# FFN of a two-layer decoder trunk: more places for the first weight parts, later first down products, later splits of kept halves, and a last tile run once

## Chip, cores and metric

The kernel runs on one core of a Trainium2 chip. The metric is the device time of one execution in microseconds (us). Five engines run their own instruction streams: TensorE (PE, with its weight loads shown as PEld), VectorE (DVE), ScalarE (ACT), GpSimd (POOL) and SyncE (SP, which here only issues DMAs). Each executes its stream in order and waits on semaphores of the others. An L with a number is a line of the kernel before, and in rows of the changed kernel a line of that.

## What is computed

One inference step of two layers, each a token mixer (an mLSTM in layer 0, latent attention over a paged cache in layer 1) followed by a SwiGLU FFN, for 1024 prompt tokens and 8 single new tokens with the same weights. All is float32. The change touches the FFN alone:

```python
def swiglu(x, w_gate_up, w_down):          # x (.., 1024), w_gate_up (1024, 5632), w_down (2816, 1024)
    g, u = jnp.split(x @ w_gate_up, 2, axis=-1)
    return (jax.nn.silu(g) * u) @ w_down
...
        hp = hp + swiglu(rmsnorm(hp, norm_ffn[layer]), ffn_w_gate_up[layer], ffn_w_down[layer])
        hs = hs + swiglu(rmsnorm(hs, norm_ffn[layer]), ffn_w_gate_up[layer], ffn_w_down[layer])
...
    y_prompt = rmsnorm(hp, norm_final)
    y_sample = rmsnorm(hs, norm_final)
```

## The kernel before

**Numbers in two halves.** Each operand of a matmul is split into a high and a low half: ACT copies it to the matmul type (L117, the hi), DVE subtracts that from the source (L118, the lo). A product is three matmuls, hi by hi (L134), hi by lo (L135) and lo by hi (L136).

**Tiles.** The 2816 hidden columns are 22 tiles f of 128, the tokens two halves i, in the matmuls 256 and 260 columns wide. The normalised input stands in SBUF as seven forms per half (sums and differences of its quarters), split too: names f0 to f7 for half 0, c0 to c5 and again f7 for half 1. `forms` makes them.

**Gate and up.** For one tile the gate and up columns together are four blocks a11, a12, a21, a22, and seven products of sums of blocks with the forms do the work of eight (`PRODUCTS`, in the order a11, a12, S2, s1, s3, a22, S4, with s1 = a21 + a22, S2 = s1 − a11, S4 = a12 − S2, s3 = a11 − a21). `operands` loads the blocks as two raw tiles of 512 KB, tag `wr`, which has two buffers. SP issues these loads at L994. POOL makes s1 (L1007), s3 (L1008), S2 in place of s1 (L1012) once s1 is split, and S4 in place of S2 (L1015) once S2 is split. Each of the seven *parts* is split into a weight tile of its own. Three places take turns: two buffers of tag `wh` and one of tag `w3`. `gate_up` runs the seven products for each token half given in `parts`, and asks `operands` for one part ahead of the one in use. A third pair, tag `wl`, stands beside `wh` in the same pool; the mixers use it, the gate and up products here do not.

**Order of the tiles.** While `forms` still makes half 1, `gate_up_half` runs tiles 0 and 1 for half 0 alone. Then `ffn` runs tile 2 for both halves, tiles 0 and 1 for half 1, and tiles 3 to 17 for both. In between it hands out the *down products* of the first 18 tiles: `down` is a generator of 504 steps, each three matmuls into banks mm and ss, with a piece of DVE or ACT work that empties a bank or prepares a next operand (b from the hidden values u; dA to dD from w_down, raw tile dr). `gate_up` has a *checkpoint* after every second group of three matmuls, 28 in a tile for both halves, and takes steps there: 2 each in tile 3 from the second checkpoint on, 1 each in the tiles behind. The two buffers `st0` of `down` have tag `wl`.

**The last four tiles** (18 to 21) are not fed to `down`: `keep` splits their hidden values (L117, out a) for `last_products`, which the end of the layer runs (`to_mla` after layer 0, `finish` after layer 1, with weight tiles wh and fw from w_down). In layer 1 tile 21 is run as two calls, one per token half, each with loads, sums and splits of its own.

A list scheduler orders the instructions of each engine when the kernel is built; on the chip that order is fixed.

Of the kernel before, what the change touches and what calls it, by code (L numbers as in the profile page):

```python
# [28 lines left out]
NF = DFF // P  # L29
# [62 lines left out]
class Kern:  # L92
# [896 lines left out]
    def operands(self, wg, f):  # L989
        nc = self.nc  # L990
        A = []
        for c0 in (f * P, DFF + f * P):
            raw = self.t(self.wp, [P, KT * P], "wr")
            nc.sync.dma_start(raw.rearrange("p (k m) -> p k m", m=P), self.wsrc(wg, 0, KT, c0, P))  # L994
            A.append(raw.rearrange("p (k r m) -> p r k m", r=2, m=P))
        (a11, a12), (a21, a22) = ((x[:, 0], x[:, 1]) for x in A)

        def put(x):
            self.no += 1
            pool, tag = (self.wp, "wh") if self.no % 3 else (self.gu, "w3")  # L1000
            w = self.t(pool, [P, KT * P], tag, F32R).rearrange("p (i k m) -> p i k m", i=2, m=P)
            self.split(w[:, 0], w[:, 1], x)
            return w

        G = nc.gpsimd.tensor_tensor
        s, s3 = (self.t(self.gu, [P, 4, P], "S", bufs=2) for i in range(2))
        G(s, a21, a22, op=ALU.add)  # L1007
        G(s3, a11, a21, op=ALU.subtract)  # L1008
        yield put(a11)
        yield put(a12)  # L1010
        s1 = put(s)
        G(s, s, a11, op=ALU.subtract)  # L1012
        yield put(s)
        yield s1
        G(s, a12, s, op=ALU.subtract)  # L1015
        yield put(s3)
        yield put(a22)
        yield put(s)


    def gate_up(self, wg, f, parts, down=iter(()), skip=0, steps=1):
        nc = self.nc
        V = nc.vector
        gu = self.gu
        banks = {}
        U, X = {}, {}
        ops = self.operands(wg, f)
        ahead = next(ops)
        for s, bank, first in PRODUCTS:
            w, ahead = ahead, next(ops, None)  # L1030
            for i in parts:
                pw = PW[i]
                if (i, bank) not in banks:
                    banks[i, bank] = self.mmt("sc")[:, :pw]
                ps = banks[i, bank]
                xh, xl = self.F[i][s]
                for k in range(4):
                    self.mm3(ps, w[:, 0, k], w[:, 1, k], xh[:, k], xl[:, k], bool(first) and k == 0, k == 3, skip_group_check=True)
                    if k % 2:
                        if skip:  # L1040
                            skip -= 1
                        else:
                            for _ in range(steps):
                                next(down, None)
                if s == 0:
                    U[i] = self.rows(f, i)
                    X[i] = self.t(gu, [P, PW[1]], "gt", bufs=2)[:, :pw]
                u, x = U[i], X[i]
                if s == 0:
                    nc.scalar.copy(u[:, 0], ps)  # L1050
                elif s == 4:
                    V.tensor_tensor(u[:, 0], u[:, 0], ps, op=ALU.add)
                    nc.scalar.activation(u[:, 0], u[:, 0], AF.Silu)
                elif s == 3:
                    nc.scalar.copy(x, ps)
                elif s == 2:
                    nc.scalar.copy(u[:, 1], ps)
                    V.tensor_tensor(u[:, 1], u[:, 1], banks[i, 1], op=ALU.add)
                elif s == 5:
                    V.tensor_tensor(u[:, 0], u[:, 0], ps, op=ALU.mult)  # L1060
                elif s == 6:
                    V.tensor_tensor(x, x, ps, op=ALU.add)
                    nc.scalar.activation(x, x, AF.Silu)
                    V.tensor_tensor(u[:, 1], u[:, 1], x, op=ALU.mult)  # L1064
# [92 lines left out]
    def ffn(self, layer):  # L1157
        wg, wd = self.ffn_w_gate_up[layer], self.ffn_w_down[layer]
        self.fp = self.pool("ffn")
        self.B = {}  # L1160
        for _, x, i in SPREAD:
            if i == 0:
                self.spread(0, x, i)
        self.gate_up(wg, 2, (0, 1))
        self.gate_up(wg, 0, (1,))
        self.gate_up(wg, 1, (1,))
        for _, x, i in SPREAD:
            if i == 1:
                self.spread(0, x, i)
        g = self.down(wd)  # L1170
        next(g)
        self.gate_up(wg, 3, (0, 1), g, 1, 2)
        for f in range(4, NF - 2):
            self.gate_up(wg, f, (0, 1), g)
        for _ in g:
            pass
        self.fp.release()
        self.fp = self.pool("ffn2")
        fs = range(NF - 4, NF)
        self.act = {f: [self.t(self.fp, [P, T], "a%d%d" % (f % 4, x), F32R) for x in range(2)] for f in fs}  # L1180

        def keep(f, i):
            o = lambda x: x[:, 512 * i:512 * i + 2 * PW[i]].rearrange("p (c t) -> p c t", c=2)
            self.split(o(self.act[f][0]), o(self.act[f][1]), self.u[f, i])

        for f in fs[:2]:
            for i in range(2):
                keep(f, i)
        for f in fs[2:]:
            for parts in ((0,), (1,)) if layer and f == NF - 1 else ((0, 1),):  # L1190
                self.gate_up(wg, f, parts)
                for i in parts:
                    keep(f, i)
        self.fc.release()
        return wd, fs

# [820 lines left out]
```

## Time and profile before

| | us |
|---|---|
| median of 3 timed runs | 2763.43 (2760.77 to 2763.75) |
| the profiled execution | 2736.87, its span 2735.1 |
| mean granted PE clock in it | 0.972 |
| tiles 2, 0, 1 of layer 0's FFN, up to the first steps of `down` | 557.1 to 617.1 |
| tile 3 of layer 0 | 617.1 to 655 |
| last tile of layer 0 (both halves at once) | 1174.0 to 1194.1 |
| tiles 2, 0, 1 of layer 1's FFN | 2023.7 to 2082.5 |
| last tile of layer 1 (half by half) | 2639.2 to 2669.8 |

A row of the profile reads: start, duration, engine, line, operation, output<-inputs by the program's names, and in brackets how long the engine stood idle before it and what ended the wait. Names stand without their numbers: `sc` is a PSUM bank of the gate and up products, `mm` and `ss` are banks of the down products, `S` is a sum that POOL makes, `wh`, `wl`, `w` (for w3) are split weight parts.

### The profile page before, as it was taken

The numbers are of one execution on the slowest core, as the hardware profiler recorded it, in microseconds if no ns is written. First come the engines' busy times: TensorE is split into PE (matmuls) and PEld (weight loads), VectorE is DVE, ScalarE is ACT, GpSimd is POOL, SyncE is SP. The second block draws the span as 40 slices with busy tenths as digits, with TensorE's granted clock in tenths as the row PEclk, the third lists the DMA queues.
The fourth block names the chain that finished last, engine by engine and source line by source line (L and its number), as shares of the span: only waits on it lengthen the run. The fifth ranks groups of instructions, "written<-read, shape, count | busy, mean of one in ns | idle before, by whom it ended". The sixth has DMA issues, their size and how long they took to land. (4 is left out here: it accounts for less than half of the span.)

```text
span 2735.1 us, 54524 instructions
## 1 busy us (share of the span) xinstructions
PE 2553.6 (93%) x21151; PEld 2398.4 (88%) x21151; DVE 1884.8 (69%) x4321; ACT 1320.8 (48%) x3287; POOL 824.9 (30%) x762
## 2 busy tenths in 40 slices
PE   8999998979999999999889889888989999999988
PEld 8998976979999999999877677677988999999988
DVE  4345668868777778666558777685676877777755
ACT  4212334446555555454345464555345555555542
POOL 1000102223333333322336454442223333333332
PEclk9999989999999999999989999899999999999999
DMA  5133454416565655643667776555424566655652
GB/s 186 39 77 89 127 147 115 154 51 128 117 129 113 132 110 112 125 154 98 229 222 270 260 261 209 202 206 168 137 71 104 113 124 127 121 117 117 128 132 102
DMA packets 344073, 384.43 MB, mean 141 GB/s; under 512 B 23449, under 2 KB 276766, under 8 KB 335494
## 3 DMA queue, kind: packets, MB, share of 16 engines
q0 software_dynamic: 59520, 183.34, 28.6%
q1 hardware_dynamic: 259894, 181.25, 22.1%
q10 hardware_dynamic: 24400, 16.36, 2.3%
q8 instruction: 166, 2.72, 0.4%
q14 instruction: 93, 0.76, 0.1%
HBM read 255.17 MB, written 125.70 MB: 139 GB/s over the span
## 5 line engine op out<-in xcount | busy, mean ns | idle before, releaser
L117 ACT ACTIVATE wh<-wr 128x512 fp32r<-128x512 f32 (+2 forms) x176 | 141.4, 804 | 224.4 <-PE mm L135 129.5
L1144 POOL DMA_DIRECT2D x_d<-wl x72 | 86.7, 1204 | 315.3 <-DVE wl L1143 250.0
L1795 DVE STREAM_TRANSPOSE tt<-nat 128x1024 f32<-128x1024 f32 x128 | 153.6, 1222 | 13.1 <-DMA nat<-in_cache_latent_dram,idx 6.9
L118 DVE TENSOR_TENSOR b<-u,b 128x256 fp32r<-128x256 f32 (+1 forms) x252 | 135.5, 542 | 16.7 <-ACT b L117 16.7
L1007 POOL TENSOR_TENSOR S<-wr 128x512 f32<-128x512 f32 x45 | 70.1, 1559 | 254.7 <-DMA wr<-in_ffn_w_gate_up_dram 230.5
L1012 POOL TENSOR_TENSOR S<-S,wr 128x512 f32<-128x512 f32 x45 | 63.0, 1401 | 245.0 <-DVE wh L118 166.2
L118 DVE TENSOR_TENSOR wl<-wr,wh 128x1024 fp32r<-128x1024 f32 (+2 forms) x83 | 99.2, 1195 | 42.7 <-ACT wh L117 30.9
L117 ACT ACTIVATE b<-u 128x256 fp32r<-128x256 f32 (+1 forms) x252 | 98.4, 415 | 43.0 <-DVE u L1060 15.4
L118 DVE TENSOR_TENSOR wh<-S,wh 128x512 fp32r<-128x512 f32 x121 | 86.2, 712 | 34.7 <-ACT wh L117 32.8
L134 PE MATMUL mm<-zh,wh 128*128 128x344 f32 x320 | 104.3, 326 | 4.2 <-DVE ot L462 4.2
L135 PE MATMUL mm<-zl,wh 128*128 128x344 f32 x320 | 103.6, 324 | 0.0
L136 PE MATMUL mm<-zh,wl 128*128 128x344 f32 x320 | 103.3, 323 | 0.0
L1144 POOL DMA_DIRECT2D x_d<-st x72 | 99.9, 1388 | 7.0 <-ACT b L117 6.1
L117 ACT ACTIVATE wh<-S 128x512 fp32r<-128x512 f32 x121 | 76.5, 633 | 48.1 <-PE sc L136 28.6
L1802 PE MATMUL ss<-tt,qbd 128*32 128x128 f32 x2560 | 88.2, 279 | 8.6 <-DVE tt L1795 7.0
L1802 PEld LDWEIGHTS ss<-tt,qbd 128*32 128x32 f32 x2560 | 70.9, 111 | 21.5 <-DVE tt L1795 15.9
L1093 DVE TENSOR_TENSOR dS<-dr 128x128 f32<-128x128 f32 x72 | 48.0, 667 | 59.4 <-DMA dr<-in_ffn_w_down_dram 56.6
L1698 PE MATMUL mm<-wh,vt 128*128 128x256 f32 (+1 forms) x320 | 76.9, 302 | 10.7 <-ACT wh L117 6.0
L134 PE MATMUL sc<-zh,wh 128*128 128x344 f32 x256 | 84.0, 329 | 0.2 <-DVE q L432 0.2
L850 POOL TENSOR_TENSOR ss<-ss,sq 128x512 f32<-128x512 f32 (+2 forms) x36 | 49.5, 1374 | 113.4 <-ACT sq L849 113.1
L135 PE MATMUL sc<-zl,wh 128*128 128x344 f32 x256 | 83.0, 324 | 0.0
L136 PE MATMUL sc<-zh,wl 128*128 128x344 f32 x256 | 82.9, 324 | 0.0
(1002 smaller groups left out, 10949.6 us busy)
## 6 DMA issues: line engine op xcount, KB each, us to landing
wr<-in_ffn_w_gate_up_dram SPq DMA_DIRECT2D x98, 512.0 KB
x_d<-st POOLq DMA_DIRECT2D x72, 520.0 KB, 8.4
x_d<-wl POOLq DMA_DIRECT2D x72, 512.0 KB, 6.2
dr<-in_ffn_w_down_dram SPq DMA_DIRECT2D x72, 256.0 KB
wr<-in_mlstm_w_in_dram SPq DMA_DIRECT2D x24, 512.0 KB
wr<-in_mlstm_w_out_dram SPq DMA_DIRECT2D x16, 512.0 KB
wr<-in_mla_w_o_dram SPq DMA_DIRECT2D x15, 512.0 KB
q<-qn_d SPq DMA_DIRECT2D x28, 256.0 KB
```

Source lines behind the costliest of these rows:

```text
L117: ins = nc.scalar.activation(hi, src, AF.Copy)
L118: self.low = e.tensor_tensor(lo, src, hi.bitcast(F32), op=ALU.subtract)
L134: mm(ps, wh, xh, start=start, stop=False, **kw)
L135: mm(ps, wh, xl, start=False, stop=False, **kw)
L136: self.last = mm(ps, wl, xh, start=False, stop=stop, **kw)
L850: (V if d == KT - 1 else nc.gpsimd).tensor_tensor(SS[:, cs], SS[:, cs], sq, op=ALU.add)
L1007: G(s, a21, a22, op=ALU.add)
L1012: G(s, s, a11, op=ALU.subtract)
L1144: nc.gpsimd.dma_start(self.x_d[:, 2 * dp:2 * dp + 2, 512 * i:512 * i + 2 * PW[i]], st[i], accum_op=ALU.add)
L1698: nc.tensor.matmul(o, x, y, start=i == 0, stop=i == len(ops) - 1)
L1795: V.transpose(out=tt, in_=src.rearrange("p s (c i) -> p c s i", i=32))
L1802: nc.tensor.matmul(psS[32 * j:32 * j + 32, u * P:u * P + P], self.qbd[:, b, cb], tt[:, c, 4 * j:4 * j + 4].rearrange("p s k -> p (s k)"), ...
```

## The change

```diff
 def operands(self, wg, f):
         def put(x):
             self.no += 1
-            pool, tag = (self.wp, "wh") if self.no % 3 else (self.gu, "w3")
+            tags = ("wh", "wl", "w3", "wh", "wl") if f < 3 else ("wh", "w3", "wh")
+            tag = tags[self.no % len(tags)]
+            pool = self.gu if tag == "w3" else self.wp
...
-    def gate_up(self, wg, f, parts, down=iter(()), skip=0, steps=1):
+    def gate_up(self, wg, f, parts, down=iter(()), skip=0, steps=(1, 1)):
...
+        cp = done = 0
         ops = self.operands(wg, f)
-        ahead = next(ops)
+        ahead = [next(ops) for _ in range(2 if f < 3 else 1)]
         for s, bank, first in PRODUCTS:
-            w, ahead = ahead, next(ops, None)
+            ahead.append(next(ops, None))
+            w = ahead.pop(0)
...
                     if k % 2:
-                        if skip:
-                            skip -= 1
-                        else:
-                            for _ in range(steps):
-                                next(down, None)
+                        cp += 1
+                        while done * steps[1] < steps[0] * (cp - skip):
+                            next(down, None)
+                            done += 1
...
-        self.gate_up(wg, 3, (0, 1), g, 1, 2)
+        self.gate_up(wg, 3, (0, 1), g, 5, (54, 23))
...
-        for f in fs[:2]:
+        for i in range(2):
+            keep(fs[0], i)
+        self.gate_up(wg, fs[2], (0, 1), (keep(fs[1], i) for i in range(2)))
+        self.gate_up(wg, fs[3], (0, 1))
+        for f in fs[2:]:
             for i in range(2):
                 keep(f, i)
-        for f in fs[2:]:
-            for parts in ((0,), (1,)) if layer and f == NF - 1 else ((0, 1),):
-                self.gate_up(wg, f, parts)
-                for i in parts:
-                    keep(f, i)
```

1. For tiles 0, 1 and 2 the parts take turns in five places (two `wh`, two `wl`, one `w3`), and two parts are asked for ahead. The tiles behind keep three places, in another phase.
2. In tile 3 the down steps start at the sixth checkpoint instead of the second: 54 of them over 23 checkpoints, spread evenly, instead of 2 at each of 27.
3. The kept halves of tile 19 are split at the first two checkpoints of tile 20's products, those of tiles 20 and 21 after both tiles.
4. Layer 1's tile 21 is run once for both halves.

In counts: PE has the same 16828 instructions, ACT and DVE 7 fewer each, POOL 4 fewer sums, SP 2 fewer loads.

The order on PE where tile 1 (second half of the tokens) ends and tile 3 begins, before: sc_6021 is a bank of tile 1, sc_6173 of tile 3.

```order
L134 MATMUL sc_6021<-f7h_5593,w_6082 128x260
L135 MATMUL sc_6021<-f7l_5594,w_6082 128x260
L136 MATMUL sc_6021<-f7h_5593,w_6082 128x260
L134 MATMUL sc_6173<-f0h_4927,wh_6167 128x256
L135 MATMUL sc_6173<-f0l_4928,wh_6167 128x256
L136 MATMUL sc_6173<-f0h_4927,wh_6167 128x256
```

And in the changed kernel, where sc_6005 is the bank of tile 1:

```order
L134 MATMUL sc_6005<-c2h_5579,wl_6037 128x260
L135 MATMUL sc_6005<-c2l_5580,wl_6037 128x260
L136 MATMUL sc_6005<-c2h_5579,wl_6037 128x260
L134 MATMUL sc_6173<-f0h_4927,w_6167 128x256
L135 MATMUL sc_6173<-f0l_4928,w_6167 128x256
L136 MATMUL sc_6173<-f0h_4927,w_6167 128x256
L134 MATMUL sc_6173<-f0h_4927,w_6167 128x256
L134 MATMUL sc_6005<-c5h_5585,wh_6053 128x260
L135 MATMUL sc_6005<-c5l_5586,wh_6053 128x260
```

Before, tile 3 began when tile 1's last product (f7) was through. Now its first four matmuls stand behind tile 1's c2 product, ahead of its last two (c5 and f7, 12 matmuls each). In the same way tile 1's first four now stand ahead of tile 0's last two.

On ACT, the start of the last four tiles in layer 0, before: a is a kept half, u at L1050 the first copy out of a bank of tile 20.

```order
L117 ACTIVATE w_13421<-S_13375 128x512
L117 ACTIVATE wh_13481<-S_13376 128x512
L117 ACTIVATE a_13355<-u_12600 128x512
L117 ACTIVATE a_13355<-u_12642 128x520
L117 ACTIVATE a_13357<-u_13006 128x512
L117 ACTIVATE a_13357<-u_13042 128x520
L1050 COPY u_13398<-sc_13385 128x256
L1050 COPY u_13414<-sc_13401 128x260
```

The same place in the changed kernel, where that copy is L1053:

```order
L117 ACTIVATE wh_13421<-S_13371 128x512
L117 ACTIVATE w_13481<-S_13372 128x512
L117 ACTIVATE a_13355<-u_12600 128x512
L117 ACTIVATE a_13355<-u_12642 128x520
L117 ACTIVATE a_13357<-u_13006 128x512
L117 ACTIVATE a_13357<-u_13042 128x520
L1053 COPY u_13398<-sc_13381 128x256
L1053 COPY u_13414<-sc_13401 128x260
```

The place of the weight parts has changed (wh and w have swapped); the four splits of kept halves stand where they stood.

On ACT, the end of layer 1 in the changed kernel: wh and fw are the weights of the last products, gt at L1066 is the last SiLU, u_31754 and u_31770 are the hidden values of tile 21 for the two halves.

```order
L117 ACTIVATE wh_31979<-wr_31977 128x512
L117 ACTIVATE wh_31986<-wr_31984 128x512
L117 ACTIVATE fw_31993<-wr_31991 128x512
L1066 ACTIVATE gt_31755<-gt_31755 128x256
L117 ACTIVATE a_31490<-u_31754 128x512
L1066 ACTIVATE gt_31771<-gt_31771 128x260
L117 ACTIVATE a_31490<-u_31770 128x520
L117 ACTIVATE fw_31999<-wr_31997 128x512
```

Before, two such splits (both wh) stood ahead of the last SiLU, which there belongs to half 1 alone, and the first fw split behind it.

One more place moves, on ACT at the start of each FFN: the first a12 split stands directly ahead of c0h, half 1's first form; before, it stood behind the sixth form.

## Prediction

> **What bounds the kernel now.** I read the busy shares of the page first, then the table of windows over the stretches that the edits touch, then what PE waits for in each, then single rows.
>
> ```profile
> span 2735.1 us, 54524 instructions
> PE 2553.6 (93%) x21151; PEld 2398.4 (88%) x21151; DVE 1884.8 (69%) x4321; ACT 1320.8 (48%) x3287; POOL 824.9 (30%) x762
> ```
>
> PE is the bound of the whole: 93% busy, 181 us of the span without a matmul. What an edit can win is PE's idle time, the time PE ran at a lower clock, or matmuls removed. None are removed, so I look for the first two. The columns are the stretch, its length, busy time of each engine (count), granted clock, DMA share and GB/s.
>
> ```profile
> core 0: us, PE busy (x) PEld busy (x) DVE busy (x) ACT busy (x) POOL busy (x), PEclk, DMA share, GB/s
> 557.10:617.10 60.00, 50.25 (x372) 48.44 (x372) 38.99 (x74) 25.40 (x60) 17.46 (x13) 0.94 0.20 58
> 617.10:655.00 37.90, 37.90 (x316) 37.70 (x317) 29.12 (x81) 26.00 (x75) 11.40 (x9) 1.00 0.70 133
> 1174.00:1194.10 20.10, 20.10 (x171) 20.10 (x170) 9.99 (x19) 8.19 (x18) 2.84 (x3) 1.00 0.20 58
> 2023.70:2082.50 58.80, 50.41 (x372) 48.79 (x372) 40.24 (x74) 25.22 (x58) 18.27 (x13) 0.92 0.22 63
> 2083.80:2087.10 3.30, 3.30 (x17) 3.30 (x17) 2.44 (x7) 1.64 (x6) 1.41 (x1) 0.50 0.00 0
> 2639.20:2669.80 30.60, 23.23 (x171) 21.99 (x170) 18.01 (x27) 13.13 (x26) 9.42 (x8) 0.94 0.56 176
> 2669.80:2690.00 20.20, 19.35 (x107) 18.00 (x106) 11.13 (x20) 9.02 (x17) 6.53 (x6) 1.00 0.41 128
> ```
>
> Row one is the start of layer 0's FFN (tiles 2, 0, 1 and the start of 3), row four the same in layer 1. Row two is tile 3, where PE never stops. Row three is layer 0's last tile, run for both halves at once; row six is layer 1's, run half by half: the same 171 matmuls in 30.6 us instead of 20.1.
>
> Unhindered, a matmul here takes 37.90/316 = 0.120 us, so the 372 of an early stretch want 44.6 us. Layer 0 spends 60.0, **15.4 more**; layer 1 spends 58.8, **14.2 more**. Part of it is clock:
>
> ```profile
> 557.10:561.40 4.30, 4.30 (x20) 4.30 (x21) 3.54 (x10) 1.72 (x6) 0.00 (x0) 0.50 0.00 0
> 602.30:605.80 3.50, 3.50 (x19) 3.50 (x18) 2.08 (x3) 0.91 (x2) 0.50 (x1) 0.51 0.48 141
> 2023.70:2029.10 5.40, 5.40 (x25) 5.40 (x26) 3.54 (x11) 2.20 (x7) 0.00 (x0) 0.50 0.15 49
> 2066.70:2070.10 3.40, 3.40 (x17) 3.40 (x17) 2.70 (x4) 1.30 (x5) 1.29 (x1) 0.50 0.06 15
> ```
>
> Half clock costs half of its length: 2.15 and 1.7 us in layer 0, 2.7 and 1.7 in layer 1, and 1.65 in the window at 2083.80 behind it. The rest is waiting; the waits of PE from 545 to 618 first, then those from 2012 to 2084 (us in total, times, longest):
>
> ```profile
> PE sc L134 <- ACT wh L117: 5.7, 3, 3.9
> PE sc L134 <- ACT w L117: 3.4, 1, 3.4
> PE mm L134 <- ACT b L117: 2.8, 1, 2.8
> PE sc L136 <- DVE wh L118: 2.7, 1, 2.7
> PE sc L136 <- DVE w L118: 1.7, 1, 1.7
> ```
>
> ```profile
> PE sc L134 <- ACT wh L117: 5.3, 3, 3.9
> PE sc L134 <- ACT w L117: 3.1, 1, 3.1
> PE sc L136 <- DVE w L118: 1.0, 1, 1.0
> ```
>
> The 3.9 and the 2.7 us stand ahead of 557.1 and 2023.7, where half 1's forms are still being made. Without them layer 0 waits 1.8 + 3.4 + 2.8 + 1.7 = 9.7 us, layer 1 1.4 + 3.1 + 2.8 (the row at 2082.45 below) + 1.0 = 8.3. What is left over (15.4 − 9.7 − 3.85 = 1.85; 14.2 − 8.3 − 4.4 = 1.5) is waits too short for the list.
>
> **Five places and two parts ahead.** Nearly all of these waits are for a hi or lo half of a weight part: a split that had no place to go to, or whose raw tile came late because the part before still held it. The first and the last of them, both for S2, and what stood behind the last:
>
> ```profile
> 565.64 0.38 PE L134 MATMUL sc<-f3h,wh 128*128 128x256 f32 x1 [0.77 <-ACT wh L117]
> ...
> 600.74 0.39 PE L134 MATMUL sc<-c3h,w 128*128 128x260 f32 x1 [3.38 <-ACT w L117]
> ```
>
> ```profile
> 595.45 1.31 POOL L1007 TENSOR_TENSOR S<-wr 128x512 f32<-128x512 f32 x1 [7.63 <-DMA wr<-in_ffn_w_gate_up_dram]
> ```
>
> Ahead of the sums that end in tile 1's S2, POOL sat idle 7.63 us for a load that went out only when the split of the tile before (its a22) had freed the raw tile. With five places that split runs while PE is still on earlier products, and the load goes out earlier: the 3.38 us and the half clock behind them (1.7) have room to go. I count all waits of the two stretches as gone but 0.5 of the 0.77 at tile 2's S2, in each layer: POOL makes that S2 from s1, whose lo half DVE reaches only after the forms, and more places don't move that.
>
> ```profile
> 617.02 0.39 PE L134 MATMUL mm<-b,dB 128*128 128x260 f32 x1 [2.83 <-ACT b L117]
> 2082.45 0.38 PE L134 MATMUL mm<-b,dB 128*128 128x260 f32 x1 [2.80 <-ACT b L117]
> ```
>
> These two go by another edit: the first down products start four checkpoints later (skip 5 for 1), and by then the last b splits of tile 1 are done. Behind the second one PE runs 3.30 us at clock 0.50 (the 2083.80 window): 1.65 more. The Trainium skill, "TensorE: Matmul & The Clock Gate", section "HAM oscillation — how this bites in real kernels", puts the danger at PE idle gaps above about 3.4 us; the trace differs, 2.80 us idle and a clock of 0.50 right after. By that rule a gap of 2 to 3 us would cost no clock, and my sum would be 1.7 us better.
>
> **What takes its place.** By the order of instructions four matmuls of tile 3 now stand ahead of the last 24 (c5, f7) of tile 1. They want tile 3's first part, whose raw load waits for S4 of tile 1:
>
> ```profile
> 580.13 1.42 POOL L1007 TENSOR_TENSOR S<-wr 128x512 f32<-128x512 f32 x1 [12.44 <-DMA wr<-in_ffn_w_gate_up_dram]
> ...
> 601.50 1.31 POOL L1015 TENSOR_TENSOR S<-wr,S 128x512 f32<-128x512 f32 x1 [1.47 <-DVE w L118]
> ```
>
> ```profile
> 576.04 0.37 SPq L994 DMA_DIRECT2D wr<-in_ffn_w_gate_up_dram  x1
> ...
> 602.83 0.37 SPq L994 DMA_DIRECT2D wr<-in_ffn_w_gate_up_dram  x1
> ```
>
> ```profile
> 600.06 0.63 ACT L117 ACTIVATE w<-S 128x512 fp32r<-128x512 f32 x1 [2.07 <-POOL S L1012]
> ```
>
> ```profile
> 600.72 0.69 DVE L118 TENSOR_TENSOR w<-S,w 128x512 fp32r<-128x512 f32 x1 [0.41 <-ACT w L117]
> ```
>
> ```profile
> 610.80 0.28 PE L134 MATMUL sc<-f0h,wh 128*128 128x256 f32 x1
> ```
>
> The load goes out as S4 ends (602.81). A load takes 4.1 us from issue to its first reader (576.04 to 580.13), the splits 0.63 and 0.69, hand-overs some 0.3: ready 5.7 us after S4. Before, PE came to tile 3 8.0 us after S4 (610.80). Now it comes 24 x 0.12 = 2.9 earlier, and 1.7 earlier without the half clock: 3.4 us after S4. So it waits **2.3 us**, and the 24 matmuls of tile 1 queue behind. Bounds: nothing, if S4 too comes earlier against PE (its own wait was part of the 3.38), and 5.7, if PE arrives as S4 ends. I take 2.3, as the rows stand. Whether the clock falls after it: of the gaps between 2.3 and 3.4 us some did (600.74, 2082.45) and one did not (617.02, followed by clock 1.00), so half of 1.7, 0.85.
>
> Sum of the early stretches. Layer 0: 9.7 − 0.5 + 1.7 − 2.3 − 0.85, and half of the 1.85 of short waits, 0.9: **8.65**. Layer 1: 8.3 − 0.5 + 1.7 + 1.65 − 2.3 − 0.85 + 0.75 = **8.75**. Bounds: nothing; and all but the clock that the forms stage leaves, 15.4 − 2.15 = 13.25 and 14.2 − 2.7 + 1.65 = 13.15.
>
> The first a12 split now stands on ACT ahead of c0h, and waits for its load there.
>
> ```profile
> 536.38 1.07 ACT L117 ACTIVATE c0h<-x 128x1040 fp32r<-128x1040 f32 x1 [3.17 <-DVE x L920]
> ```
>
> ACT is idle 3.17 us there anyway, so 0.63 fits in, if the load has landed; else c0h, and all forms behind it, come late by up to half a us per layer. DVE has work of its own then; I take 0.25 each, **0.5**.
>
> **Last tile for both halves.** Layer 1's goes from 30.6 us to the form that layer 0 has, 20.1: **10.5**, with the waits (PE busy 23.23 of 30.60), the part of the clock below 1.00 and the second preparation of the seven parts gone (7 splits on ACT and on DVE, 4 sums on POOL, 2 loads). Behind it stand 20.2 us of last products with 0.85 idle. ACT's order there now has three w_down splits ahead of the last SiLU; they need loads that the shorter tile brings nearer. Bounds: 0.85 better, 2.5 worse (the last SiLU's u is needed for the last products, and two loads may not be there); I take 0.
>
> **The rest.** Tile 3 hands out 54 down steps over 23 checkpoints, 2.35 each for 2. Before, it ran them without an idle us (37.90 of 37.90), with DVE at 29.12/37.90 = 77%; at 2.35 that is about 84%: nothing, as long as DVE stays below PE. From tile 4 on the ring of three only changes phase: 7 parts per tile already pass all phases. Nothing. Splitting the kept halves later was to be felt at the first of the last four tiles:
>
> ```profile
> 1158.12 0.39 PE L134 MATMUL sc<-f3h,w 128*128 128x256 f32 x1 [3.12 <-ACT u L1050]
> ```
>
> PE waits here for a copy that stands behind four kept splits on ACT. By the order of instructions the same four splits stand ahead of it after the change, so I count nothing; were it gone, 3.1 us in each layer and a half clock would be won.
>
> Sum: 8.65 + 8.75 + 10.5 − 0.5 = **27.4**. The profiled execution takes 2736.87 us (span 2735.1), and would take 2709.5. The median of the runs shown is 2763.43, 1% above; the waits counted are in us and not in shares, so I take 27 from it: **2736**.
>
> **Rivals.**
> - Loads and POOL's sums set the pace of the early tiles, not places. For it: POOL's 7.63 us idle for a load, and a raw ring that stays at two. Against: a load takes 4.1 us, so 7.63 us are not the load alone. Then only the last tile gains: 2763 − 10.5 = 2753. Chance 0.12.
> - No new wait at tile 3, and the forms' clock all that is left: 13.25 + 13.15 + 11.35 = 37.7, 2726. Against: the 24 matmuls moved. Chance 0.06.
> - It does little: the early tiles gain nothing, and in the last tile the SiLU waits behind splits whose loads are late. Against: layer 0's 20.1 us. 2758 to 2763. Chance 0.05.
> - **Slower:** DVE becomes the bound of tile 3. At 2.35 steps a checkpoint PE would stop for banks that DVE has not emptied. It decides once a step costs over 27.4/108 = 0.25 us more than now (54 steps, two layers), at 0.35 us the time is 2774. Against: the 77%, and full windows at 2 steps. Chance 0.03.
>
> **How the numbers follow.** The forecast has 0.74. Its own range is 2728 to 2748 (a gain of 15 to 35). The range takes in the first rival: 2728 to 2754, which leaves out 2726, the small and the slower case, 0.14. Faster by over 0.2% (5.5 us, about what a measurement of this kernel can tell from no change): 0.74 + 0.12 + 0.06 = 0.92, and I take 0.91; same 0.06; slower 0.03.
>
> **What would show it.** Right: an early stretch of about 51 us from PE's restart (557.1) to the same count of matmuls; no PE wait above 1 us for S2 of tile 1; one of 2 to 3 us at tile 3's first matmuls, for ACT or DVE; no b wait at the start of the down products; tile 3 full; a last tile of 20 us in layer 1; the waits at 1158 and 2625 still there. Wrong: POOL still idle for loads as long as before, PE waiting for DVE within tile 3, or the last products grown by more than 2.5 us.

## The result, and the profile after

Timed side by side on one chip, the changed kernel takes 2735.09 us (median of 8 runs, 2729.94 to 2753.23), the kernel before 2762.44 (8 runs): 27.3 us less by the medians, 24.8 by the means, ratio 0.991, 95% interval 0.9887 to 0.9933. Two later jobs give 0.9915 (0.989 to 0.994) and 0.9904 (0.9881 to 0.9928).

The two profiled executions do not show this distance: their spans are 2735.1 and 2729.4. The first lines of the page after:

```profile
span 2729.4 us, 54469 instructions
PE 2547.4 (93%) x21151; PEld 2388.5 (88%) x21151; DVE 1869.7 (69%) x4314; ACT 1315.5 (48%) x3280; POOL 820.7 (30%) x758
```

(PE's count is 21151 in both; the 16828 named with the change is found in neither profile.) The distance is hidden by code that neither kernel changes. From the end of layer 0's last tile to the end of half 0's products in layer 1 (all of the attention) the trace of before takes 820.8 us, that of after 841.7: 20.9 more. What stands ahead of half 0's last product in layer 0 took 548.1 us there and 543.4 here, 4.7 less, and 543.4 to 552.1 over all traces below. In the attention stage the difference goes with the job, and each job had one chip: 818 to 827 us in two jobs, 840 to 848 in a third, whatever the kernel. So the stages of the FFN are compared one by one, and times only within a job.

The windows of the profile after that answer to those of before: the early stretch of layer 0 and tile 3 behind it, the early stretch of layer 1 and a half clock in it, layer 1's last tile and the first 20 us of the last products behind it.

```profile
core 0: us, PE busy (x) PEld busy (x) DVE busy (x) ACT busy (x) POOL busy (x), PEclk, DMA share, GB/s
552.60:606.00 53.40, 49.40 (x377) 47.71 (x378) 36.12 (x77) 25.41 (x60) 18.10 (x13) 0.96 0.23 65
606.00:640.00 34.00, 33.75 (x284) 33.54 (x283) 25.74 (x70) 22.12 (x64) 11.40 (x9) 1.00 0.73 143
2033.30:2087.60 54.30, 51.01 (x378) 49.66 (x379) 36.70 (x80) 25.77 (x59) 18.61 (x14) 0.92 0.24 69
2072.80:2076.20 3.40, 3.40 (x17) 3.40 (x18) 3.06 (x7) 2.04 (x5) 0.00 (x0) 0.50 0.55 162
2645.00:2665.10 20.10, 20.10 (x171) 20.10 (x170) 10.20 (x19) 8.87 (x19) 2.86 (x3) 1.00 0.64 197
2665.10:2685.20 20.10, 19.90 (x113) 19.18 (x112) 11.35 (x21) 9.18 (x18) 6.19 (x6) 1.00 0.47 146
```

The reader is to see three things. The last tile has layer 0's form, 20.10 us without a gap, 10.5 less than 30.60. The early stretches are shorter, but not full: by the starts of the matmuls, 372 of them from PE's restart take 52.8 us in layer 0 (59.9 before) and 53.5 in layer 1 (58.8 before), 7.2 and 5.3 less. And tile 3 is full, 33.75 of 34.00.

What PE waits for in layer 0 from 553 to 612, after (the 4.4 stands at the restart, ahead of the stretch):

```profile
PE sc L136 <- DVE wl L118: 4.6, 2, 4.4
PE sc L134 <- ACT u L1053: 2.1, 2, 1.6
PE sc L134 <- DVE u L1055: 0.7, 1, 0.7
PE sc L134 <- DVE u L1061: 0.5, 1, 0.5
PE sc L136 <- DVE w L118: 0.3, 1, 0.3
PE sc L134 <- ACT wl L117: 0.2, 1, 0.2
```

Before, PE waited for weight parts (wh, w) and for b. Those lines are nearly gone. Of those within the stretch the longest is new: ACT u L1053, the copy that empties a bank. Single rows of PE after show where it is; the third is the place where a wait of 2.3 us was forecast, the last two are tile 1 in layer 1 and the start of the last four tiles:

```profile
591.45 0.39 PE L134 MATMUL sc<-c3h,wh 128*128 128x260 f32 x1 [1.65 <-ACT u L1053]
593.83 0.39 PE L134 MATMUL sc<-c1h,w 128*128 128x260 f32 x1 [0.69 <-DVE u L1055]
597.54 0.38 PE L136 MATMUL sc<-f0h,w 128*128 128x256 f32 x1 [0.31 <-DVE w L118]
...
2072.63 0.50 PE L134 MATMUL sc<-c3h,wh 128*128 128x260 f32 x1 [2.03 <-ACT u L1053]
...
1145.29 0.58 PE L134 MATMUL sc<-f3h,wh 128*128 128x256 f32 x1 [3.13 <-ACT u L1053]
```

The first two are tile 1's third and fourth products. The third product (S2) adds into the bank that the first (a11) has filled, so it needs the split of S2 and also the copy that takes the first product out of that bank. ACT's rows just before 591.45 tell why the copy is late:

```profile
588.65 0.63 ACT L117 ACTIVATE wh<-S 128x512 fp32r<-128x512 f32 x1 [2.56 <-POOL S L1014]
589.19 0.40 ACT L117 ACTIVATE b<-u 128x260 fp32r<-128x260 f32 x1
589.50 0.61 ACT L117 ACTIVATE wl<-S 128x512 fp32r<-128x512 f32 x1
590.71 0.42 ACT L1066 ACTIVATE gt<-gt 128x260 f32<-128x260 f32 x1 [0.60 <-DVE gt L1065]
591.04 0.36 ACT L1053 COPY u<-sc 128x260 f32<-128x260 f32 x1
```

In ACT's order the copy stands behind the split of S2, which waits 2.56 us for POOL, and behind three more instructions. ACT is through with S2 at 589.28, 1.8 us before the copy starts.

S2 itself comes late on POOL. The rows of POOL that begin tile 0's and tile 1's sums (half 1), after:

```profile
568.13 1.31 POOL L1009 TENSOR_TENSOR S<-wr 128x512 f32<-128x512 f32 x1 [5.78 <-DMA wr<-in_ffn_w_gate_up_dram]
...
584.12 1.31 POOL L1009 TENSOR_TENSOR S<-wr 128x512 f32<-128x512 f32 x1 [6.51 <-DMA wr<-in_ffn_w_gate_up_dram]
```

Before, POOL was idle 12.44 and 7.63 us ahead of these two. Counted from half 0's last product, tile 1's sums start at 40.7 us instead of 47.3. So the loads do come earlier, but POOL still waits for them.

### The profile page after: what moved, and what is told of

Same layout as the page of the kernel before. It is cut to its first block, busy times and chain, and to the rows that moved or that the text cites. A ratio compares the mean times of both kernels' runs of the same rounds, so it can differ in the third digit from the quotient of the medians.

```text
span 2729.4 us, 54469 instructions
## 1 busy us (share of the span) xinstructions
PE 2547.4 (93%) x21151; PEld 2388.5 (88%) x21151; DVE 1869.7 (69%) x4314; ACT 1315.5 (48%) x3280; POOL 820.7 (30%) x758
## 4 chain that ended last, share of the span: by engine, by line
PE 57%; DVE 22%; DMA 10%; ACT 5%; issue 3%; POOL 1%; SPq 1%; another core or an unknown queue 0%; ACTq 0%; DVEq 0%; POOLq 0%
PE sc L134 10%; PE sc L136 10%; PE sc L135 10%; PE mm L134 4%; PE mm L136 4%; PE mm L135 4%; DVE b L118 3%; PE ss L1829 2%; DVE tt L1797 2%; DMA Gb<-G_d 2%; DVE wl L118 2%; DMA dr<-in_ffn_w_down_dram 2%; PE ss L1804 1%; PE ss L134 1%; PE ss L136 1%
## 5 line engine op out<-in xcount | busy, mean ns | idle before, releaser
L118 DVE TENSOR_TENSOR b<-u,b 128x256 fp32r<-128x256 f32 (+1 forms) x252 | 128.6, 515 | 11.6 <-ACT b L117 11.5
L1804 PE MATMUL ss<-tt,qbd 128*32 128x128 f32 x2560 | 91.7, 278 | 15.4 <-DVE tt L1797 10.5
L118 DVE TENSOR_TENSOR wh<-S,wh 128x512 fp32r<-128x512 f32 x108 | 74.8, 693 | 25.4 <-ACT wh L117 24.2
L117 ACT ACTIVATE wh<-S 128x512 fp32r<-128x512 f32 x108 | 68.4, 633 | 45.8 <-PE sc L136 29.0
L118 DVE TENSOR_TENSOR wh<-wr,wh 128x512 fp32r<-128x512 f32 x85 | 64.0, 753 | 27.7 <-ACT wh L117 26.3
```

The source lines that it names most:

```text
L117: ins = nc.scalar.activation(hi, src, AF.Copy)
L118: self.low = e.tensor_tensor(lo, src, hi.bitcast(F32), op=ALU.subtract)
L1804: nc.tensor.matmul(psS[32 * j:32 * j + 32, u * P:u * P + P], self.qbd[:, b, cb], tt[:, c, 4 * j:4 * j + 4].rearrange("p s k -> p (s k)"), ...
```

## The experiments

Stage lengths of every trace, worked out from the starts of PE's matmuls. Early: from the last product of half 0 (the start of its last matmul, in the forms stage) to the end of tile 1. FFN: from the same start to the end of the last tile, so the early stretch is part of it. Attention: what lies between the two FFNs.

| kernel | early, layer 0 / 1 | FFN, layer 0 / 1 | last tile, layer 1 | attention |
|---|---|---|---|---|
| before | 62.5 / 61.5 | 645.8 / 655.0 | 30.5 | 820.8 |
| before again | 62.4 / 62.0 | 648.3 / 656.0 | 31.5 | 823.4 |
| last tile alone | 62.2 / 62.1 | 644.4 / 642.6 | 19.9 | 819.9 |
| places alone | 56.9 / 59.7 | 639.7 / 652.2 | 31.4 | 825.7 |
| down later alone | 62.3 / 60.9 | 642.8 / 653.5 | 31.3 | 821.0 |
| after | 57.2 / 58.2 | 638.7 / 641.1 | 20.0 | 841.7 |
| after again | 57.2 / 57.6 | 641.3 / 638.5 | 20.0 | 846.6 |
| after, third | 57.6 / 58.1 | 638.9 / 638.3 | 20.0 | 819.6 |
| after, down as before | 58.0 / 57.6 | 637.8 / 640.1 | 20.0 | 848.3 |
| copy ahead of keep | 57.5 / 59.7 | 635.5 / 637.8 | 20.0 | 840.3 |
| copy ahead, again | 59.7 / 57.6 | 637.5 / 635.9 | 20.0 | 818.3 |
| raw places | 57.0 / 57.0 | 639.2 / 638.7 | 20.0 | 848.0 |
| four places | 56.4 / 59.4 | 634.9 / 641.0 | 20.0 | 825.8 |
| low half on POOL | 55.2 / 57.2 | 631.7 / 634.5 | 20.0 | 827.3 |

Layer 0's FFN is the same code in the first three rows and takes 644.4 to 648.3 us: one trace settles no difference below some 4 us there.

### The kernel before again

No edit.

> The kernel before, unchanged, for a second trace of it. Theory: the profiled execution of before (2736.87 us) was 20 us quicker than usual in code that the change does not touch, the attention over the cache between 1450 and 1900 us, so a second trace takes 2757 to 2764 us, spends about 20 us more there, and shows the same FFN stages within 1 us each (the early stretch of 60 us, the last tile of 30.6 us). Rival: the FFN stages themselves vary, and a second trace shows them 5 us or more shorter or longer.

Measured: 2737.01 us (12 runs) against 2735.15 of its own runs beside it, ratio 1.0001 (0.9985 to 1.0018). It did not take the 2757 to 2764 us of the theory, and its attention stage is as short as in the first trace, 823.4 us. The theory fell: the short attention stage was no chance of one execution. What the record has in its place is the job, and with it the chip: in this job before takes 2735 us, in the first job it took 2762. The FFN stages were within 1 us, but for tile 3 and what follows in layer 0 (2.5 us longer).

### The last tile alone

```diff
         for f in fs[2:]:
-            for parts in ((0,), (1,)) if layer and f == NF - 1 else ((0, 1),):
-                self.gate_up(wg, f, parts)
-                for i in parts:
-                    keep(f, i)
+            self.gate_up(wg, f, (0, 1))
+            for i in range(2):
+                keep(f, i)
```

> Before, with layer 1's last tile run once for both halves and nothing else. Theory (the parts add up): 10.5 to 11.6 us less, a ratio of about 0.996; the tile takes 20 us. Rival: the w_down loads, which the shorter tile brings nearer, make the last products wait and give half of it back: 5 us less, ratio 0.998.

Measured: 2723.71 us, ratio 0.9957 (0.9942 to 0.9972), 11.8 us less (7.7 to 15.9). The tile takes 19.9 us. The theory stands; the last products do not give it back.

### The places alone

```diff
-            pool, tag = (self.wp, "wh") if self.no % 3 else (self.gu, "w3")
+            tags = ("wh", "wl", "w3", "wh", "wl") if f < 3 else ("wh", "w3", "wh")
+            tag = tags[self.no % len(tags)]
+            pool = self.gu if tag == "w3" else self.wp
...
-        ahead = next(ops)
+        ahead = [next(ops) for _ in range(2 if f < 3 else 1)]
...
-            w, ahead = ahead, next(ops, None)
+            ahead.append(next(ops, None))
+            w = ahead.pop(0)
```

> Before, with five places for the parts of tiles 0 to 2 and two parts asked for ahead, and nothing else; the order on PE then no longer has down products among the products of tiles 2, 0 and 1. Theory: this is most of the gain of the early stretches, 5 to 6 us in layer 0 and 4 to 5 in layer 1, with a wait for b of up to 2.8 us left at the first down products: 10 us less, ratio 0.9965. Rival (loads and POOL's sums set the pace): under 3 us in both together, ratio 0.999.

Measured: 2723.05 us, ratio 0.9946 (0.9933 to 0.9958), by which it is 14.8 us less (11.5 to 18.3); the medians differ by 12.1, and the FFN stages by 10.7. The rival (under 3 us) fell, and with it the prediction's first rival, by which the early tiles gain nothing. With the 11.8 us of the last tile alone, this makes up nearly the whole effect. The waits of PE from 558 to 652 in this kernel (the first line is the restart at 557.42 and a short one):

```profile
PE sc L136 <- DVE wl L118: 4.9, 2, 4.7
PE sc L134 <- ACT u L1053: 1.9, 2, 1.5
PE sc L134 <- DVE u L1055: 0.7, 1, 0.7
PE sc L134 <- DVE u L1061: 0.5, 1, 0.5
PE sc L134 <- ACT wl L117: 0.4, 1, 0.4
PE mm L134 <- ACT st L1141: 0.3, 1, 0.3
```

There is no wait for b, though the down steps start where they did; the theory had up to 2.8 us of it left. The places take that one too: the order no longer moves down products in among those of tiles 2, 0 and 1, and the first ones come when b is split. The bank copy's wait (ACT u) is already there, so it comes with the places. In the trace the early stretches give 5.6 us in layer 0 and 1.8 to 2.3 in layer 1, where a half clock comes in.

Asking for two parts ahead, the other half of this edit, changes no order by itself: with one part ahead the order of the changed kernel is the same, row for row, on all five engines but for the names of the places. It was not run alone.

### The later down steps alone

```diff
-        self.gate_up(wg, 3, (0, 1), g, 1, 2)
+        self.gate_up(wg, 3, (0, 1), g, 5, (54, 23))
```

with the new counting of checkpoints.

> Before, with the down steps of tile 3 started four checkpoints later and spread evenly, and nothing else. Theory: the two waits for b (2.83 and 2.80 us) go, with the half clock behind the second (1.65): 5 to 7 us less, ratio 0.998. Rival: PE waits as long for the first parts of tile 3, which its products reach earlier: within 2 us of before, ratio 1.000.

Measured: 2738.47 us, ratio 1.0015 (1.0002 to 1.0028): no gain, 0.5 to 7.7 us slower. The waits from 600 to 652:

```profile
PE sc L134 <- ACT w L117: 3.1, 1, 3.1
PE ss L134 <- DVE st L1134: 1.8, 1, 1.8
```

The 2.83 us for b are gone as the theory said, and another wait has come: a down bank (ss) that DVE has not emptied yet, 1.8 us, once in each layer. That is the mechanism of the prediction's slower rival, small and in one place. The rival's own words (a wait for tile 3's first parts) were not what happened. The stage lengths of this trace show no loss, so the 4 us of the time are not placed.

### The changed kernel again, and with the down steps as before

```diff
-        self.gate_up(wg, 3, (0, 1), g, 5, (54, 23))
+        self.gate_up(wg, 3, (0, 1), g, 1, (2, 1))
```

> The changed kernel, unchanged, beside the three that follow, and for a second trace of it. Theory: by the traces so far the parts add up to 21 to 25 us (layer 0's early tiles 8, layer 1's 3.5 to 5, the last tile 10.5 to 11.5), so the ratio to before is 0.991 to 0.992 again, whatever the chip. Rival: the 27 us of the first measurement came with its chip, and here the ratio is 0.994 or above.

> The changed kernel with the down steps of tile 3 as before (from the second checkpoint, two each). Theory: five places alone have already taken away the waits for b, so the later start brings nothing: within 2 us of the changed kernel, and PE does not wait for b at the first down products. Rival (the prediction's): the waits for b come back, 2.8 us in each layer, and the time is 5 us longer.

Measured in one job: before 2760.95, the changed kernel 2735.41 (0.9915, 0.989 to 0.994), with the down steps as before 2739.69 (0.9928, 0.9901 to 0.9956). No wait for b came back, so the rival fell. The 4.3 us between the two have overlapping intervals and do not show in the FFN stages (1277.9 us in both layers together against 1279.8): open. The changed kernel's own ratio is the one that the theory gave; its rival, 0.994, is the end of the interval.

### The bank copies ahead of the kept splits

```diff
-        x = self.t(self.gu, [P, 2, PW[1]], "u%d%d" % ((1, 0) if (f, i) == (0, 1) else (f % 2, i)))[:, :, :PW[i]]
+        if f >= NF - 2:
+            x = self.t(self.fp, [P, 2, PW[1]], "v%d%d" % (f % 2, i))[:, :, :PW[i]]
+        else:
+            x = self.t(self.gu, [P, 2, PW[1]], "u%d%d" % ((1, 0) if (f, i) == (0, 1) else (f % 2, i)))[:, :, :PW[i]]
...
-        for i in range(2):
-            keep(fs[0], i)
-        self.gate_up(wg, fs[2], (0, 1), (keep(fs[1], i) for i in range(2)))
+        self.gate_up(wg, fs[2], (0, 1), (keep(f, i) for f in fs[:2] for i in range(2)), 12)
```

> The changed kernel, where tiles 20 and 21 keep their hidden values in places of their own, so that the first bank copies of tile 20 need not wait until the halves of tile 18 are split; on ACT both copies now stand ahead of the four splits. Theory: the 3.1 us that PE waits there in each layer fall to about 1 (the copy follows the split of s3, which itself waits for PE), and the half clock behind them (3.4 to 6.8 us long) goes: 5 to 9 us less than the changed kernel. Rival: the next thing is just as late (the kept splits on DVE, a weight part), and it is 2 us or less.

> The kernel of the copies ahead of the kept splits once more, for its distance to the changed kernel: 4 to 7 us less again (two waits of 3.13 us that fall to 1.04, 4.2 us, and two to four half clocks less that cost 1.7 each); rival: the 6 us of the first time were chance, and it is under 3.

Measured: 2729.17 us beside 2735.41 of the changed kernel (ratios to before 0.9892, 0.9864 to 0.9919, and 0.9915); on another chip 2705.65 beside 2707.93 (0.9897, 0.9871 to 0.9923, and 0.9904): 6.2 and 2.3 us less. PE at tile 20 in the two layers, and ACT in layer 0:

```profile
1153.29 0.39 PE L134 MATMUL sc<-f3h,wh 128*128 128x256 f32 x1 [1.04 <-ACT v L1056]
...
2631.39 0.39 PE L134 MATMUL sc<-f3h,wh 128*128 128x256 f32 x1 [1.04 <-ACT v L1056]
```

```profile
1152.34 0.63 ACT L117 ACTIVATE w<-S 128x512 fp32r<-128x512 f32 x1 [2.22 <-PE sc L136]
1152.88 0.63 ACT L1056 COPY v<-sc 128x256 f32<-128x256 f32 x2
1153.40 1.17 ACT L117 ACTIVATE a<-u 128x512 fp32r<-128x512 f32 x2
```

3.13 us became 1.04, and no half clock follows in either layer; in the trace of the changed kernel of the same job both waits had one. So the edit that was to split kept halves later could not work by its place alone: by the program, tile 20 writes into the buffers that hold tile 18's values, and its copy has to wait for tile 18's two splits. The other two splits ahead of it are tile 19's, which no buffer holds there. The experiment gave tile 20 buffers of its own and also handed out all four splits later, and no run separates the two. The first job lies in the range of its theory, the second in that of its rival; by the FFN stages it is 6.5 us less in the first and 3.8 in the second. Between them lie the 4.2 us of the waits, and more than that is not shown.

### Raw tiles of their own for tile 1

```diff
         for c0 in (f * P, DFF + f * P):
-            raw = self.t(self.wp, [P, KT * P], "wr")
+            if f == 1:
+                raw = self.t(self.fp, [P, 2, 2 * PW[1]], "st", bufs=2).rearrange("p r t -> p (r t)")[:, :KT * P]
+            else:
+                raw = self.t(self.wp, [P, KT * P], "wr")
```

> The changed kernel, where the two raw tiles of tile 1 go into the two st buffers of the down products, idle until then, so that its loads need not wait for tile 0's S4. Theory: the supply chain (load, POOL's sums, ACT's split, and the bank copy behind it) sets the wait at tile 1's third product; its S2 comes about 3 us earlier, the wait there (1.65 and 2.03 us) falls under 0.5, the half clock behind it in layer 1 goes: 3 to 6 us less than the changed kernel. Rival: the copy stands behind the SiLU of tile 0, which waits for PE and DVE, and the wait stays above 1.2 us: within 1.5 us of the changed kernel.

Measured: 2740.72 us, 0.9931 (0.9906 to 0.9956), beside 2735.41: no gain (the intervals overlap, and the FFN stages are 1277.9 us together against 1279.8). The wait at the third product is gone, and the fourth waits instead:

```profile
600.97 0.39 PE L134 MATMUL sc<-c1h,w 128*128 128x260 f32 x1 [1.69 <-DVE u L1058]
```

DVE's rows ahead of it:

```profile
598.56 1.42 DVE L1078 TENSOR_TENSOR u<-u 128x260 f32<-128x260 f32 x1
599.90 0.68 DVE L118 TENSOR_TENSOR wh<-st,wh 128x512 fp32r<-128x512 f32 x1
600.51 0.41 DVE L1058 TENSOR_TENSOR u<-u,sc 128x260 f32<-128x260 f32 x1
```

And POOL's row beside the first of them:

```profile
598.26 1.43 POOL L1012 TENSOR_TENSOR S<-wr 128x512 f32<-128x512 f32 x1 [0.62 <-DVE wl L118]
```

The theory fell, and so did its rival, which had the wait stay where it was: the third product's wait went, 1.65 and 0.69 became nothing and 1.69. The add that empties the second bank stands on DVE behind a sum for b and a weight split. About 1 us of the 1.69 is no matter of order: that sum took 1.42 us beside a POOL sum, where the same sum took 0.43 in the changed kernel of this job. With earlier loads DVE is the next limit, by its order and by POOL's work beside it, and it is as late within a us. Which of the two decides was not tested.

### Four places

```diff
-            tags = ("wh", "wl", "w3", "wh", "wl") if f < 3 else ("wh", "w3", "wh")
+            tags = ("wh", "wl", "wh", "wl") if f < 3 else ("wh", "w3", "wh")
```

> The changed kernel with four places (two wh, two wl) for tiles 0 to 2 instead of five. Theory: what is left in these tiles is the order on ACT and DVE and the supply of tiles 0 and 1, which run for one token half; places no longer bind, so the stretch from forms to the end of tile 1 stays at 57 to 58.5 us and the time within 2 us of the changed kernel. Rival: places still bind, the stretch grows by 2 us or more in each layer and the time by 4.

> The changed kernel once more, beside the three that follow. Theory: its FFN stages take what they took before (61.5 to 62.5 us less half clocks from forms to the end of tile 1 in no layer: 57 to 58.5; last tile 20.0), and the attention stage between the two FFNs takes 820 to 826 us or 840 to 848 us with the chip, for both kernels alike, so that the ratio stays at 0.991 to 0.992 on either. Rival: on a chip where before takes 2735 us the changed kernel gains less, ratio 0.994 or above.

Measured in one job: before 2734.16, the changed kernel 2707.93 (0.9904), with four places 2714.43 (0.9931, 0.9911 to 0.9952). By time the fifth place is worth 6.5 us, though the intervals overlap. The traces divide: layer 0's early stretch is 1.2 us shorter with four places, layer 1's 1.3 longer, with this wait for the same bank copy and a half clock behind it:

```profile
2055.64 0.53 PE L134 MATMUL sc<-c3h,wh 128*128 128x260 f32 x1 [3.47 <-ACT u L1053]
```

The FFN stages of the two traces are 1275.9 us with four places and 1277.2 with five, so the 6.5 us do not show there. Whether the fifth place matters stays open. What this job settles is that the gain does not hang on the attention stage: the changed kernel spends 819.6 us in it here, as the two traces of before do, and gains as much as where it takes 840.

### The low half of tile 2's first parts on POOL

On top of the kernel with the copies ahead:

```diff
-        def put(x):
+        def put(x, lo=False):
...
-            self.split(w[:, 0], w[:, 1], x)
+            self.split(w[:, 0], w[:, 1], x, lo_eng=nc.gpsimd if lo else None)
...
-        yield put(a11)
+        yield put(a11, f == 2)
         yield put(a12)
-        s1 = put(s)
+        s1 = put(s, f == 2)
```

> The kernel of the copies ahead of the kept splits, where POOL instead of DVE makes the lo halves of tile 2's first part (a11) and of its s1. In the changed kernel the hi of a11 is ready at 540.2 us, and its lo waits on DVE behind the forms until 552.5, while POOL idles; PE waits 2.65 and 4.41 us there and then runs 10 us at half clock. Theory: the two waits fall to about 3 us together and tile 2 starts 3 to 4 us earlier: 6 to 12 us less than the kernel without it. Rival: POOL and DVE hold each other up while both work (a POOL sum took 2.97 us instead of 1.31 there), the forms end later by what is won: within 2 us.

Measured: 2703.71 us, 0.9882 (0.9854 to 0.9909), beside 2705.65 without it: 1.9 us less, as the rival has it. The FFN stages say otherwise: 1266.2 us together against 1273.4, 7.2 less, which is in the theory's range; the attention stage took 9.0 us longer in this trace than in that one. With one trace each, and intervals that overlap, what the edit is worth stays open. PE's start of tile 2:

```profile
549.68 0.39 PE L136 MATMUL sc<-f0h,wl 128*128 128x256 f32 x1 [1.42 <-POOL wl L118]
553.37 0.39 PE L134 MATMUL sc<-c4h,w 128*128 128x260 f32 x1 [0.54 <-DVE u L980]
556.64 0.58 PE L134 MATMUL sc<-c3h,wl 128*128 128x260 f32 x1 [2.77 <-ACT u L1056]
559.33 0.58 PE L136 MATMUL sc<-f4h,w 128*128 128x256 f32 x1 [1.89 <-DVE w L118]
```

Tile 2 starts 2.3 us after half 0's last product instead of 9.2, and the 7.1 us of waiting (2.65 and 4.41) come back as 6.6 in four pieces: the forms and the bank copies behind them are now what is late. In POOL's and DVE's rows both slow each other there:

```profile
549.57 2.30 POOL L118 TENSOR_TENSOR wh<-S,wh 128x512 fp32r<-128x512 f32 x1
551.96 2.16 POOL L1017 TENSOR_TENSOR S<-S,wr 128x512 f32<-128x512 f32 x1
```

```profile
547.25 1.23 DVE L923 TENSOR_TENSOR x<-x 128x1040 f32<-128x1040 f32 x1
```

```profile
550.65 2.32 DVE L923 TENSOR_TENSOR x<-x 128x1040 f32<-128x1040 f32 x1
553.23 1.98 DVE L923 TENSOR_TENSOR x<-x 128x1040 f32<-128x1040 f32 x1
```

The single row is the same instruction in the changed kernel with POOL idle, 1.23 us; beside POOL's work it takes 2.32 and 1.98. The Trainium skill, "SBUF — State Buffer", section "SBUF: two separate sides", calls the port pair that the two engines share an exclusive lock for a whole instruction, where DVE reads two inputs from SBUF; the rows do not speak against it, as 1.1 and 0.75 us more are no longer than one POOL sum (1.31). This kernel has the lowest median of the study, but its distances to the one without it (1.9 us) and to the changed kernel (4.2) are not beyond the noise.

## Why the prediction was right, and where it was not

The forecast was 27 us less from three terms; 27.3, 25.5 and 26.2 were measured. By the table, the mean of the traces of after (639.6 and 639.3) stands 7.4 and 16.2 us under that of the two of before (647.1 and 655.5), and the end behind the last tile is 1.1 shorter (65.7 to 64.6): 24.7 together. So the three gains are there, the two early ones smaller than forecast, and the sum is 2.7 us high by the stages. That the medians of the first job agree with it to a few tenths is luck: their means differ by 24.8, and 23.4 and 24.7 in the later jobs. The terms, one by one:

- **Last tile, 10.5: right.** 30.6 to 20.1 us, 11.8 (7.7 to 15.9) alone. The three w_down splits ahead of the last SiLU cost nothing that shows. The 20.2 us of last products in the prediction are a window, not the stage: from the last tile's last matmul to the last of these 288 matmuls it took 53.8 and 54.3 us in the traces of before and 52.5 to 53.2 in those of after.
- **Early stretches, 8.65 and 8.75: too high.** Against the means of the two traces of before (59.7 and 58.9), the three traces of after (52.8, 52.5 and 53.0; 53.5, 53.0 and 53.6) give 6.7 to 7.2 and 5.3 to 5.9. The step "all waits of the two stretches as gone but 0.5" held for the weight parts. What it missed is a wait for a bank: in the first trace 1.65 + 0.69 + 0.47 + 0.42 us in layer 0, and 2.03 + 0.63 + 0.41 in layer 1 with a half clock (1.7) where I had counted half of one. That half clock is chance: the second trace waits 1.89 us at the same matmul and has none.
- **The new wait of 2.3 us at tile 3's first products: wrong.** It was 0.31 us there, and nothing in layer 1 of that trace. S4 of tile 1 ended at about 591.5 and tile 3's part was ready at 597.54, 6.0 us later (5.7 forecast). But PE had been held 1.65 + 0.69 = 2.3 us for the bank ahead of it, and so came 2.3 us later, when the part was nearly ready. So the chain to tile 3's part was worked out rightly, and hidden by another wait in front of it. That the two sizes agree is luck, as they have different causes. The step that failed is what PE meets on its way there: my chain followed load, POOL, splits and left out that the copy out of the bank queues on ACT behind the late split of S2. The experiment with raw tiles bears it out: with S2 earlier the wait for that copy is gone.
- **"These two go by another edit": wrong.** The waits for b went with the places alone. The later start alone took them too, but brought the 1.8 us for the down bank and no time. In the changed kernel it is not shown to be worth anything.
- **a12 ahead of c0h, 0.25 each: the size is right, the cause not shown.** From half 0's last product to PE's restart it took 8.9 or 9.0 us in both traces of before, and 9.2 to 9.5 in those of after. No run moves a12 alone, and with four places it took 8.3.
- **The kept halves, nothing: right**, 3.13 against 3.12 us, but I had put it down to ACT's order alone. By the program the buffer holds half of that order in place, and the experiment that changed both took the wait down to 1.04.
- **Tile 3 at 2.35 steps, nothing: right in this kernel** (33.75 of 34.00), not in the kernel with three places, where 1.8 us came.
- **The profiled execution "would take 2709.5": not met as it stands.** The trace of after took 2731.15 us, with the long attention stage; in the job with the short one the changed kernel's median is 2707.93.

On the clock: the Trainium skill, "TensorE: Matmul & The Clock Gate", section "HAM oscillation — how this bites in real kernels", puts the danger at idle gaps above about 3.4 us; the traces went on against it. Behind the 2.03 us of layer 1 the clock was 0.50 for 3.4 us (the window at 2072.80). The 1.65 us in layer 0 had no such stretch behind them. So a gap of 2 to 3 us has a chance of half clock, as the prediction had priced it, and no certainty: the 3.12 or 3.13 us at the start of tile 20, the same wait in 22 places of 11 traces, met half clock in 16 of them.

## What to carry to other kernels

When a wait for an operand is taken away, ask at the same matmul for its other condition: the bank it writes must have been emptied, and the instruction that empties it may stand, in order, behind the very split that was late. An agreement of the sum says little of its terms, so look at each. An edit that only writes a piece of work later does not move it if a shared buffer forces it to come first; look for the buffer, too. And before two profiles are subtracted, compare a stage that neither kernel changes: here it differed by 21 us between two executions, nearly as much as the whole effect.

## What was not expected of the hardware

- One stage, the attention over the paged cache, took 818 to 827 us in the traces of two jobs and 840 to 848 in those of a third, in the same code. Each job had one chip; whether it is the chip or where the data lies on it, and what in the stage is slower, is not shown.
- PE gaps of about 2 us were followed by half clock, and not always: 1.78 us in the kernel with the down steps as before (clock 0.50 from 596.20 to 599.60, row below) and 2.03 us as above were; 1.65, 1.74 and 1.87 us at the same matmul of layer 0 in the three traces of the changed kernel were not. The length of the gap alone does not decide it.

```profile
596.20:599.60 3.40, 3.40 (x17) 3.14 (x16) 2.49 (x6) 1.78 (x5) 0.00 (x0) 0.50 0.66 194
```

- POOL's two-input sums nearly doubled a DVE instruction beside them (1.23 to 2.32 us) and were themselves slowed (a sum of 1.31 us took 2.16): moving DVE's work to POOL won the place in the order and lost part of it in speed.
